# Decay rows as whole runs in DRAM, and a new work list for layer 1 of a two-layer hybrid trunk

## The chip, the cores and the metric

The kernel runs on one core of a Trainium2 chip. The metric is device time in microseconds (us), the median of several runs. A core has five engines with an instruction queue each: TensorE (PE) multiplies matrices into PSUM, VectorE (DVE) and ScalarE (ACT) do elementwise work, GpSimd (POOL) does elementwise work on SBUF alone, and SyncE (SP) here only issues DMAs. Every queue is worked off in order: an instruction that waits holds up all that stand behind it on its engine.

## What is computed

The reference runs 640 tokens (a prompt of 128 and a sample of 512) of width 1024 through two layers and a final norm. Each layer normalises, modulates by a condition, runs one mixer and adds its gated output to the stream.

```python
for i in range(DEPTH):
    ...
    hp = rms_norm(yp, norm_g[i]) * (1.0 + sc_p) + sh_p
    hs = rms_norm(ys, norm_g[i]) * (1.0 + sc_s) + sh_s
    if i % N_MIXERS == 0:
        out_p, out_s = conformer_branch(hp, False, *cw), conformer_branch(hs, True, *cw)
    else:
        out_p, s_f, s_b = ssd_branch(hp, zero_state, zero_state, *sw)
        out_s, _, _ = ssd_branch(hs, state_fwd[:, j], state_bwd[:, j], *sw)
    yp = yp + gt_p * out_p
    ys = ys + gt_s * out_s
```

Layer 1, where the change lies, is a Mamba-2 scan in both directions, in chunks of 128 tokens (one of the prompt, four of the sample) with 32 heads in 4 groups:

```python
a_cum = jnp.cumsum(la, axis=-1)
lower = jnp.tril(jnp.ones((CHUNK, CHUNK), dtype=bool))
seg = a_cum[..., :, None] - a_cum[..., None, :]
decay_mat = jnp.exp(jnp.where(lower, seg, -jnp.inf))
cb = jnp.einsum('bclgn,bcsgn->bcgls', cc, bc)
y_diag = jnp.einsum('bcgrls,bcsgrp->bclgrp', cb[:, :, :, None] * decay_mat, xdt)
chunk_states = jnp.einsum('bcsgn,bcgrs,bcsgrp->bcgrpn', bc, decay_to_end, xdt)
y_off = jnp.einsum('bclgn,bcgrpn,bcgrl->bclgrp', cc, prev, jnp.exp(a_cum))
```

The decay matrix needs, for each chunk and group, the running sum of every head as a row that all partitions see, and the same sum as a column.

## The kernel before

Layer 0 (the convolution branch) takes the first half of the time. Layer 1 then works through 38 projection tiles in an order that PLAN1 writes out: x (16 tiles, two of which layer 0 already does), B and C (4 each) and z (16). Each tile is 48 matmuls of 128x128 by 320 columns; the weights are split into a high and a low half to keep float32 accuracy, so each product is three matmuls. After its projection an x, B or C tile is evacuated by ScalarE, convolved with 5 taps (ScalarE the first, VectorE four), passed through SiLU and, for x and B, turned by TensorE so that tokens lie on partitions. Behind the projections the scan of a group starts: "group" needs B and the four x tiles of its group. Its chains in the two directions ("chain") multiply x by weights on GpSimd (xw), make a chunk's state on TensorE (pst), and add it to the state decayed by GpSimd (stn). Each chunk's output needs the product of C and B (pcb), the decay matrix (gf), their product on VectorE, TensorE's py, and the contribution of the states (po, yo). Gating by z, a split into halves (yh, yl), a sum of squares (ysq, ssp) and the output products follow; "o" items of PLAN1 are the output products of groups 0 to 2, and "last_products" those of group 3, followed by the final norm and the store.

The decay matrix is loaded rather than computed: the running sums of both directions lie in DRAM as acd, 128 rows (direction and head) by 384 columns. "decays" (L1575 to L1595) loads for each group and chunk 8 rows, spread over 64 partitions by a broadcast: gf takes 128 columns of each row, gb 64. So the pieces are 512 and 256 bytes long. There are four DMAs per chunk, 20 chunks in all. "decay" then subtracts a column from gb on GpSimd (L1567), copies half of it into gf under a mask on VectorE (L1569), and takes the exponential on ScalarE (L1573).

The order of all instructions of a layer is made when the program is built. Every chain of work is a generator that yields steps: "op" names an engine, a duration and the function that emits the instructions; "key" waits for another chain's mark; "get" and "put" take and return buffers of a ring. The class Order (L244) keeps a clock for each engine, picks among the chains' next steps the one that can begin first (with a priority per kind of chain, PRIO1, for ties), emits it and advances the clock. Some steps name two engines; the first way is taken at its time, the other with a bias:

```python
key = (t + 0.4 * load if len(ways) == 1 else t + dur - ways[0][1] + bias * n, ch[2], ch[3])
...
t = yield either((PO, 1.29, lambda: G.tensor_add(out=x_, in0=x_, in1=as_part(tmp, ch))), (VL, 0.66, lambda: V.tensor_add(out=x_, in0=x_, in1=as_part(tmp, ch))), bias=PRIO1["add_way"] * 0.2)
```

A step on SP counts as done LATE = 4.2 us after its issue. A clock for the transfers (DM) exists, and layer 1 does not use it. Rings say how many buffers there are: two for gf and gb each, six for the states (st).

Of the kernel before, what the change touches and what calls it, by code (L numbers as in the profile page):

```python
# [13 lines left out]
P = 128  # L14
# [36 lines left out]
def trunk(ctx: ExitStack, tc: tile.TileContext, a: dict):  # L51
# [194 lines left out]
    class Order:  # L246
        def __init__(self, prio):
            self.clock = [0.0] * 6
            self.table = None
            self.port = 0.0  # L250
            self.keys = {}
            self.rings = {}
            self.chains = []
            self.count = 0
            self.prio = prio
            self.same = [-OVER[e_] for e_ in range(5)]
            self.same.append(0.0)
            self.lead = MARGIN[PE]
            self.dirty = True
# [50 lines left out]
        def run(self, until=None):  # L310
            while self.chains:
# [26 lines left out]
                ch[1] = t + dur + LATE.get(eng, 0.0)  # L338
# [9 lines left out]
    LATE = {SP: 4.2}  # L348
# [828 lines left out]
    if True:  # L1177
# [22 lines left out]
        acd = dr.tile([P, 384], F32, name="acd")  # L1200
# [37 lines left out]
        def w_load(i, src, g=None):  # L1238
# [35 lines left out]
            t = yield op(SP, 0.35, load)  # L1274
# [57 lines left out]
        def convolve(ps, j, tag, bufs, name, cell, u=None):  # L1332
# [9 lines left out]
            for d in range(1, 5):  # L1342
                t = yield op(VL, 0.89, lambda: V.scalar_tensor_tensor(out=acc, in0=u[:, d : d + PW], scalar=c("w_c", j * 5 + d), in1=acc, op0=ALU.mult, op1=ALU.add))  # L1343
# [144 lines left out]
        def gate_loads():  # L1488
            yield key(("gated",))
            for g in range(3):  # L1490
                for hf in range(2):
# [7 lines left out]
                    t = yield op(SP, 0.6, load)  # L1499
# [12 lines left out]
            t = yield op(SP, 1.2, load_last)  # L1512
# [64 lines left out]
        def decays():  # L1577
            yield key(("cols",))
            for g in range(NG):
                for n, ch in enumerate(ORDER[g]):  # L1580
# [4 lines left out]
                    def load():  # L1585
# [3 lines left out]
                        for z_, n_, flip in ((gb, 64, True), (gf, 128, False)):  # L1589
                            for i in range(2):  # L1590
                                r, col = at(i != flip, ch, 8 * g)
                                col += 64 * (flip and i)
                                nc.sync.dma_start(out=z_[64 * i : 64 * i + 64].rearrange("p (h n) -> p h n", h=8), in_=acd[r : r + 8, col : col + n_].unsqueeze(0).broadcast_to([64, 8, n_]))
                    t = yield op(SP, 4.0, load)
                    start(decay(g, n, *tiles, t), t)  # L1595

        def group(g):
# [13 lines left out]
            for back, ch0, nm in ((0, 1, "st_f"), (1, 4, "st_b")):  # L1611
# [5 lines left out]
                t = yield op(SP, 0.4, load)  # L1617
# [43 lines left out]
            def prompt():  # L1661
                yield key(("pc", g, 0), ("st", g, 0, 4), ("st", g, 1, 3))
                for back in range(2):
# [10 lines left out]
                    t = yield op(SP, 0.1, lambda: nc.sync.dma_start(out=a["o_st"][back, g], in_=cell[1]))  # L1674
# [59 lines left out]
            for n, ch in enumerate(order):  # L1734
# [118 lines left out]
        def out_weights():  # L1853
# [13 lines left out]
            yield op(SP, 0.1, load)  # L1867
# [14 lines left out]
            t = yield op(SP, 0.3, load_gain)  # L1882
# [90 lines left out]
        def time_steps():  # L1973
# [47 lines left out]
        def rows_out():  # L2021
            yield op(SP, 0.1, lambda: nc.sync.dma_start(out=acd, in_=rp))
# [215 lines left out]
```

## Time and profile before

| | |
|---|---|
| runs | 1068.51, 1068.78, 1073.05 us; median 1068.78 |
| the profiled execution | 1068.35 us; its span from first to last instruction 1066.6 us |
| busy share of the span | PE 97%, PEld 89%, DVE 76%, ACT 62%, POOL 45% |
| matmuls | 7473 |
| DMA | 151.62 MB in 99162 packets, 29168 of them under 512 bytes |
| layer 1's projections on PE | from 544.9 us on |
| mean granted clock of TensorE | 0.991 |

The profile is of one execution. "Busy" sums the time in which an engine had an instruction in work; PE is matmul, PEld the load of its stationary operand, which overlaps. A matmul is shown from its start to the end of its way through the array, so its length is more than the distance to the next. A row of waits gives the waiting engine and line, what ended the wait, and then the total in us, the number of times and the longest. A row of DMA issues gives how long the queue took to issue; "landing" is from issue to the data's arrival. In a row of stretches each engine's busy us is followed by its number of instructions, and at the end stand TensorE's granted clock, the busy share of the 16 DMA engines and GB/s.

### The profile page before, as it was taken

Reading aid. Unit: us, or ns where it says so; the run is one execution under the profiler, and the core shown is the slowest. Engines: PE = TensorE matmul, PEld = TensorE weight load, DVE = VectorE, ACT = ScalarE, POOL = GpSimd, SP = SyncE. Lnnn points to the kernel's source line nnn. Section 1 sums busy time; section 2 is a strip of 40 time slices with the busy share of each in tenths; the row PEclk is TensorE's granted clock in tenths of the full one; section 3 lists DMA queues with packets and bytes.
Section 4 is the critical chain, followed back from the end, with each engine's and each line's share of the span. In section 5 each row is a group of like instructions: output and inputs, shape, how many; then the busy total and the mean of one; then the engine's idle time right before and its main releaser. Section 6 shows DMA issues by size and latency. Waiting matters only on the chain.

```text
span 1066.6 us, 19151 instructions
## 1 busy us (share of the span) xinstructions
PE 1033.6 (97%) x7473; PEld 948.5 (89%) x7473; DVE 807.8 (76%) x1214; ACT 666.5 (62%) x1109; POOL 478.1 (45%) x474
## 2 busy tenths in 40 slices
PE   6999999999999999999999999999999999999986
PEld 3899999999999999999999988997889778997665
DVE  2599999998997689103779788887769767965797
ACT  6468788787686678333587756774637533852454
POOL 0029999978596501111000147326561576006732
PEclk9999999999999999999999999999999999999988
DMA  9598788788766667675122753333553534335323
GB/s 359 195 256 206 190 218 198 178 210 210 176 141 137 141 136 155 150 168 123 60 76 61 156 120 103 86 101 84 144 138 98 120 88 120 84 109 134 97 69 92
DMA packets 99162, 151.62 MB, mean 142 GB/s; under 512 B 29168, under 2 KB 62336, under 8 KB 99072
## 3 DMA queue, kind: packets, MB, share of 16 engines
q1 hardware_dynamic: 87280, 118.15, 38.0%
q0 software_dynamic: 8640, 30.94, 17.3%
q10 hardware_dynamic: 3152, 1.31, 0.5%
q8 instruction: 59, 0.97, 0.4%
q14 instruction: 31, 0.25, 0.1%
HBM read 145.45 MB, written 4.92 MB: 141 GB/s over the span
## 4 chain that ended last, share of the span: by engine, by line
PE 88%; DVE 6%; DMA 2%; ACT 2%; issue 1%; SPq 0%; DVEq 0%; ACTq 0%
PE pz L1299 9%; PE o L1550 8%; PE xs L1299 7%; PE C L1299 3%; PE po L1692 3%; PE pst L1629 2%; PE B L1299 2%; PE py L1760 2%; PE o L1904 1%; PE o__4958 L157 1%; PE o__5245 L157 1%; PE o__5267 L157 1%; PE o__5258 L157 1%; PE o__5238 L157 1%; PE o__4948 L157 1%; DMA wa<-w_ada 1%
## 5 line engine op out<-in xcount | busy, mean ns | idle before, releaser
L809 DVE SCALAR_TENSOR_TENSOR cva<-v,cst,cva 128x550 f32<-128x550 f32 (+12 forms) x346 | 270.1, 821 | 11.4 <-ACT cva L801 6.3
L881 POOL TENSOR_TENSOR cv<-cv,tp 128x490 f32<-128x490 f32 (+5 forms) x134 | 172.6, 1288 | 8.5
L840 ACT ACTIVATE tp<-v,cst 128x490 f32<-128x490 f32 (+5 forms) x134 | 92.4, 718 | 36.3 <-POOL cv L881 35.9
L424 ACT CAST wh<-wf 128x1024 fp32r<-128x1024 f32 x63 | 65.9, 1046 | 63.5 <-PE o__5267 L157 30.0
L1299 PE MATMUL pz<-h_hi,wh 128*128 128x320 f32 x256 | 85.6, 334 | 0.8 <-ACT up L1330 0.8
L1299 PE MATMUL pz<-h_hi,wl 128*128 128x320 f32 x256 | 79.8, 312 | 0.1
L1299 PE MATMUL pz<-h_lo,wh 128*128 128x320 f32 x256 | 79.7, 311 | 0.0
L1529 POOL TENSOR_TENSOR x<-x,tmp 128x512 f32<-128x512 f32 x30 | 45.1, 1506 | 70.8 <-DVE tmp L1525 70.7
L1299 PE MATMUL xs<-h_hi,wh 128*128 128x320 f32 x224 | 76.0, 339 | 0.0
L1698 POOL TENSOR_TENSOR y<-y,yo 128x512 f32<-128x512 f32 x32 | 47.3, 1477 | 58.2 <-DVE yo L1696 51.4
L1573 ACT ACTIVATE gf<-gf,cols 128x128 f32<-128x128 f32 x160 | 50.8, 390 | 32.3 <-DVE gf L1569 32.2
L1343 DVE SCALAR_TENSOR_TENSOR xs<-up,cst,xs 128x642 f32<-128x642 f32 x64 | 62.9, 984 | 9.6 <-ACT xs L1341 7.9
L1299 PE MATMUL xs<-h_hi,wl 128*128 128x320 f32 x224 | 69.2, 309 | 0.0
L1299 PE MATMUL xs<-h_lo,wh 128*128 128x320 f32 x224 | 69.1, 308 | 0.0
L434 ACT ACTIVATE wl<-wh 128x1024 fp32r<-128x1024 f32 x58 | 61.5, 1061 | 1.7
L435 POOL DMA_DIRECT2D wl<-w_in x43 | 37.5, 872 | 54.8 <-ACT wl L434 51.6
L1256 DVE TENSOR_TENSOR wl<-wf,wh 128x1024 fp32r<-128x1024 f32 x38 | 49.9, 1317 | 15.5 <-ACT wh L1248 11.9
L1567 POOL TENSOR_TENSOR gb<-gb,cols 128x512 f32<-128x512 f32 x20 | 24.5, 1223 | 71.6 <-DVE C L1343 63.2
L1550 PE MATMUL o<-wh,yh 128*128 128x512 f32 x120 | 54.0, 450 | 0.0
L435 POOL DMA_DIRECT2D wl<-w_out x15 | 13.0, 865 | 90.4 <-ACT wl L434 90.4
L1299 PEld LDWEIGHTS pz<-h_hi,wh 128*128 128x128 f32 x256 | 48.6, 190 | 3.9 <-issue 2.6
L1299 PEld LDWEIGHTS pz<-h_lo,wh 128*128 128x128 f32 x256 | 48.8, 190 | 2.1 <-issue 1.9
(848 smaller groups left out, 3518.6 us busy)
## 6 DMA issues: line engine op xcount, KB each, us to landing
wf<-w_in SPq DMA_DIRECT2D x48, 512.0 KB, 3.8
wl<-w_in POOLq DMA_DIRECT2D x43, 512.0 KB, 7.3
wa<-w_ada SPq DMA_DIRECT2D x64, 256.0 KB, 6.0
wf<-w_out SPq DMA_DIRECT2D x32, 512.0 KB, 3.6
wf<-w_xbc SPq DMA_DIRECT2D x24, 512.0 KB, 4.0
gf<-acd SPq DMA_DIRECT2D x40, 256.0 KB, 4.9
wa<-w_ada SPq DMA_DIRECT2D x16, 512.0 KB, 10.2
wf<-w_z SPq DMA_DIRECT2D x16, 512.0 KB, 3.6
```

What stands on the lines that cost most here:

```text
L157: T.matmul(ps[:, b, at : at + t1 - t0], lhsT=w, rhs=h[:, t0:t1], start=first and n == 0, stop=last and n == 2)
L424: t = yield op(ACT, 1.05, lambda: S.copy(out=wh, in_=wf))
L434: yield op(ACT, 1.06, lambda: S.activation(out=wl, in_=wh.bitcast(F32), func=AF.Copy, scale=-1.0))
L435: t = yield op(PD, 0.7, lambda: G.dma_start(out=wl, in_=src, accum_op=ALU.add))
L809: t = yield op(VE, 0.24 + 0.01 * (hi - lo), lambda: V.scalar_tensor_tensor(out=rows64(accs[i], lo, hi), in0=rows64(vs[i], lo + d, hi + d), ...
L840: t = yield op(ACT, 0.72, lambda: S.activation(out=tp[:, :, 0 : hi - lo], in_=rows64(vs[i], lo + d, hi + d), func=AF.Copy, scale=w_dw(i, t ...
L881: t = yield op(PO, 1.3 + 0.019 * (hi - lo - 49), lambda: G.tensor_add(out=rows64(cv[i], lo, hi), in0=rows64(cv[i], lo, hi), in1=sgs["tp", ...
L1256: e_.tensor_sub(out=cell["wl"], in0=cell["wf"], in1=cell["wh"].bitcast(F32))
L1299: T.matmul(ps[:, b, at_ : at_ + t1 - t0], lhsT=w_, rhs=t_[:, t0:t1], start=k == 0 and n == 0, stop=k == nk - 1 and n == 2)
L1343: t = yield op(VL, 0.89, lambda: V.scalar_tensor_tensor(out=acc, in0=u[:, d : d + PW], scalar=c("w_c", j * 5 + d), in1=acc, op0=ALU.mult, ...
L1550: T.matmul(ps, lhsT=t_, rhs=w_, start=k == 0 and n == 0, stop=k == 3 and n == 2)
L1573: t = yield op(ACT, 0.39, lambda: S.activation(out=gv[:, h_, :], in_=gv[:, h_, :], func=AF.Exp, bias=cols1[ch][:, o8 + h_ : o8 + h_ + 1]), ...
```

## The change

The running sums are written to DRAM twice: acf holds three blocks (the chunk's place in a row) of 128 rows by 128 columns, acb three blocks of two halves of 128 rows by 64 columns. The 8 rows of a group are then one contiguous run of 4 KB in acf and of 2 KB in acb, and each partition's share of a load is one piece. Bytes and the number of loads stay; the one write becomes two.

Layer 1's list now uses the transfer clock: most loads name a time on it as a last argument, and the lateness of SP steps is 2.6 us in layer 1 (layer 0 keeps 4.2). A chunk's loads count 1.5 us on SP and 2.2 on the transfer clock, in the place of 4.0 us on SP. Several VectorE durations are raised (a convolution step from 0.89 to 0.97). The subtraction that makes the low half of a gained weight, two instructions, is listed as two steps. TensorE's margin is a knob and comes out as before, 0.2 x (-2 + 7) = 1.0 us. There is one buffer for gb, and seven for the states. All of PRIO1 and PLAN1 are new; they were chosen by replaying the finished order with scattered durations. Among the priorities, add_way goes from 5 to -3, so the bias of the residual adds goes from +1.0 to -0.6.

```diff
-PLAN1 = "z00 b0 z01 x03 x02 c0 x11 x10 z02 x13 x12 b1 x20 x23 z03 x22 z10 c1 b2 o00 z11 x33 o01 c2 z12 x21 z13 z20 b3 z30 o10 z21 o11 z22 z23 x30 x32 c3 x31 z31 o20 z32 o21 z33"
-RB1 = {"xs": 2, "st": 6, "gf": 2, "gb": 2}
+PLAN1 = "z00 b0 c0 z01 x02 x03 x13 b1 x10 x12 x22 x11 z02 x20 c1 x23 z03 b2 z10 x21 o00 z11 x33 o01 z12 z13 z20 c2 z30 x30 z21 x32 o10 z22 c3 z23 z31 o11 b3 x31 o20 z32 o21 z33"
+RB1 = {"xs": 2, "st": 7, "gf": 2, "gb": 1}
...
+            self.late = 4.2
...
-                ch[1] = t + dur + LATE.get(eng, 0.0)
+                ch[1] = t + dur + (self.late if eng == SP else 0.0)
                 if table and eng != ACT:
                     self.clock[DM] = max(self.clock[DM], t + 0.3) + table
                     ch[1] = max(ch[1], self.clock[DM] + (2.2 if eng == SP else -3.6))
...
-        acd = dr.tile([P, 384], F32, name="acd")
+        acf = dr.tile([3, P, 128], F32, name="acf")
+        acb = dr.tile([3, 2, P, 64], F32, name="acb")
...
-                    t = yield op(VL, 1.55, lambda: low(V))
+                    yield op(VL, 0.77, lambda: low(V))
+                    t = yield op(VL, 0.77, lambda: low(V, 1))
...
-            t = yield op(SP, 0.35, load)
+            t = yield op(SP, 0.35, load, 1.35)
...
-                        for z_, n_, flip in ((gb, 64, True), (gf, 128, False)):
-                            for i in range(2):
-                                r, col = at(i != flip, ch, 8 * g)
-                                col += 64 * (flip and i)
-                                nc.sync.dma_start(out=z_[64 * i : 64 * i + 64].rearrange("p (h n) -> p h n", h=8), in_=acd[r : r + 8, col : col + n_].unsqueeze(0).broadcast_to([64, 8, n_]))
-                    t = yield op(SP, 4.0, load)
+                        for i in range(2):
+                            r, col = at(1 - i, ch, 8 * g)
+                            nc.sync.dma_start(out=gb[64 * i : 64 * i + 64], in_=acb[col // 128, i, r : r + 8, :].rearrange("h n -> (h n)").unsqueeze(0).broadcast_to([64, 512]))
+                        for i in range(2):
+                            r, col = at(i, ch, 8 * g)
+                            nc.sync.dma_start(out=gf[64 * i : 64 * i + 64], in_=acf[col // 128, r : r + 8, :].rearrange("h n -> (h n)").unsqueeze(0).broadcast_to([64, 1024]))
+                    t = yield op(SP, 1.5, load, 2.2)
...
-            yield op(SP, 0.1, lambda: nc.sync.dma_start(out=acd, in_=rp))
+            yield op(SP, 0.4, lambda: nc.sync.dma_start(out=acb.rearrange("c f p n -> p c f n"), in_=rp.rearrange("p (c f n) -> p c f n", c=3, f=2)), 1.0)
+            yield op(SP, 0.4, lambda: nc.sync.dma_start(out=acf.rearrange("c p n -> p c n"), in_=chunks(rp)), 0.8)
...
-            run.clock = [0.0, -2.0, -2.0, -2.0, -9.0]
+            run.clock = [0.0, -2.0, -2.0, -2.0, -9.0, -9.0]
+            run.lead = 0.2 * (PRIO1["lead"] + 7)
+            run.late = 2.6
```

More of the change, by code (lines that the diff above doesn't have):

```diff
@@ L1251, in high, with low @@
                         S.activation(out=cell["wh"][:, z_], in_=cell["wf"][:, z_], func=AF.Copy, scale=sn)
-            def low(e_):
-                cell["wl"] = gp.tile([P, 1024], F32R, tag="wl", bufs=3, name="wl")
+            def low(e_, n=0):
+                if n == 0:
+                    cell["wl"] = gp.tile([P, 1024], F32R, tag="wl", bufs=3, name="wl")
                 if g is None:
@@ L1257, in low @@
                 else:
-                    for z_, sn in gained(g, cell):
-                        e_.scalar_tensor_tensor(out=cell["wl"][:, z_], in0=cell["wf"][:, z_], scalar=sn, in1=cell["wh"][:, z_].bitcast(F32), op0=ALU.mult, op1=ALU.subtract)
+                    (z_, sn), = gained(g, cell)[n : n + 1]
+                    e_.scalar_tensor_tensor(out=cell["wl"][:, z_], in0=cell["wf"][:, z_], scalar=sn, in1=cell["wh"][:, z_].bitcast(F32), op0=ALU.mult, op1=ALU.subtract)
             def split():
@@ L1279, in gained @@
         def gained(g, cell):
-            for n in range(2):
-                yield slice(n * 512, n * 512 + 512), c("sn_g", g + n)
+            return [(slice(n * 512, n * 512 + 512), c("sn_g", g + n)) for n in range(2)]
         def w_chain():
@@ L1342, in convolve @@
             for d in range(1, 5):
-                t = yield op(VL, 0.89, lambda: V.scalar_tensor_tensor(out=acc, in0=u[:, d : d + PW], scalar=c("w_c", j * 5 + d), in1=acc, op0=ALU.mult, op1=ALU.add))
+                t = yield op(VL, 0.97, lambda: V.scalar_tensor_tensor(out=acc, in0=u[:, d : d + PW], scalar=c("w_c", j * 5 + d), in1=acc, op0=ALU.mult, op1=ALU.add))
             up_free(u, t)
@@ L1673, in prompt @@
                     put("b", t)
-                    t = yield op(SP, 0.1, lambda: nc.sync.dma_start(out=a["o_st"][back, g], in_=cell[1]))
+                    t = yield op(SP, 0.35, lambda: nc.sync.dma_start(out=a["o_st"][back, g], in_=cell[1]))
                     put("st", t)
@@ L1743, in group @@
                 cbd = lp.tile([P, 1], F32, tag="cbd", bufs=2, name="cbd")
-                yield op(VE, 0.4, lambda: V.scalar_tensor_tensor(out=pcb[:, 128:256], in0=pcb[:, 0:128], scalar=1.0, in1=eye, op0=ALU.mult, op1=ALU.mult, accum_out=cbd))
+                yield op(VE, 0.3, lambda: V.scalar_tensor_tensor(out=pcb[:, 128:256], in0=pcb[:, 0:128], scalar=1.0, in1=eye, op0=ALU.mult, op1=ALU.mult, accum_out=cbd))
                 co = lp.tile([P, 8], F32, tag="co", bufs=2, name="co")
-                t = yield op(VL, 0.25, lambda: V.scalar_tensor_tensor(out=co, in0=cols2[ch][:, 96 + o8 : 104 + o8], scalar=cbd, in1=c("d", o8, 8), op0=ALU.mult, op1=ALU.add))
+                t = yield op(VL, 0.36, lambda: V.scalar_tensor_tensor(out=co, in0=cols2[ch][:, 96 + o8 : 104 + o8], scalar=cbd, in1=c("d", o8, 8), op0=ALU.mult, op1=ALU.add))
                 start(other_y(ch, co, n), t)
@@ L1866, in out_weights @@
             yield get("wf")
-            yield op(SP, 0.1, load)
+            yield op(SP, 0.35, load, 1.35)
             for k in range(2):
```

15 lines of the change are left out of this document (7 added, 8 removed).

## The prediction

> **What bounds the kernel now.** I read the page first, then the busy time by stretches, then TensorE's waits in the part that the change touches.
>
> ```profile
> span 1066.6 us, 19151 instructions
> PE 1033.6 (97%) x7473; PEld 948.5 (89%) x7473; DVE 807.8 (76%) x1214; ACT 666.5 (62%) x1109; POOL 478.1 (45%) x474
> ```
>
> ```profile
> core 0: us, PE busy (x) PEld busy (x) DVE busy (x) ACT busy (x) POOL busy (x), PEclk, DMA share, GB/s
> 1057.90:1066.60 8.70, 0.00 (x0) 0.00 (x0) 2.96 (x6) 2.37 (x6) 1.27 (x1) 0.66 0.43 121
> 0.00:545.00 545.00, 533.14 (x4409) 514.51 (x4409) 400.94 (x608) 363.99 (x540) 264.09 (x309) 1.00 0.71 176
> 545.00:1000.00 455.00, 449.06 (x2813) 395.72 (x2814) 348.13 (x496) 268.56 (x495) 187.62 (x144) 1.00 0.42 109
> 1000.00:1067.00 67.00, 51.41 (x254) 38.24 (x252) 58.69 (x112) 33.90 (x75) 26.35 (x22) 0.90 0.33 91
> ```
>
> TensorE is the bound, and the span splits at 545 us, where layer 1's list begins. From there to 1000 us TensorE is idle for 455.00 - 449.06 = 5.9 us. From 1000 us on it is idle for 15.6 us, of which 8.7 us lie behind its last matmul (the final norm and the store), so 6.9 us are gaps; its clock there is 0.90. All that a better list can win lies in these gaps and in that clock. The waits name them:
>
> ```profile
> PE ssp L1830 <- DVE ysq L1825: 2.6, 2, 1.4
> PE ptx L1367 <- ACT xs L1345: 1.2, 1, 1.2
> ```
>
> ```profile
> PE ssp L1830 <- DVE ysq L1825: 1.5, 1, 1.5
> PE pst L1629 <- DVE yo L1696: 1.3, 1, 1.3
> PE py L1760 <- DVE gf L1751: 1.2, 2, 0.6
> PE ssp L1830 <- ACT ss L1838: 1.2, 1, 1.2
> PE pcb L1740 <- ACT xt L1730: 0.7, 1, 0.7
> ```
>
> The first two rows are from 545 to 1000 us, the other five from 1000 us on. No row names a DMA: the transfers that the change speeds up reach TensorE only through VectorE or ScalarE.
>
> **The change part by part.**
>
> *Layer 0* keeps its priorities, plan and lateness of 4.2: no change up to 545 us.
>
> *The decay transfers.* Four DMAs per chunk, twenty chunks:
>
> ```profile
> L1593 SPq DMA_DIRECT2D gb<-acd x40: 580/621/1307, 597.9 to 1011.2; - x40
> L1593 SPq DMA_DIRECT2D gf<-acd x40: 573/626/1713, 599.3 to 1012.5; - x40
> L2022 SPq DMA_DIRECT2D acd<-room x1: 327/327/327, 578.0 to 578.0; - x1
>   POOL gb L1567: 8.4, 6
>   ACT L1573: 5.3, 2
> DMA to landing us min/median/max: 1.9/4.9/9.8
> ```
>
> ```profile
> 597.00:611.00 14.00, 14.00 (x99) 13.93 (x98) 9.59 (x13) 9.58 (x19) 1.32 (x2) 1.00 0.99 197
> 956.00:962.00 6.00, 6.00 (x28) 4.82 (x27) 1.55 (x3) 0.27 (x1) 3.23 (x3) 1.00 0.47 175
> ```
>
> ```profile
> L1243 SPq DMA_DIRECT2D wf<-w_z x15: 327/333/2846, 545.5 to 972.3; - x15
> ```
>
> GpSimd and ScalarE waited 8.4 and 5.3 us for these landings. In the stretch with two decay chunks the DMA engines are full (0.99) and move 197 GB/s, so 199 GB/s at a share of one. In the second stretch, where only whole rows of 2 and 4 KB move, it is 175 / 0.47 = 372 GB/s. A chunk is 2 x 256 + 2 x 128 = 768 KB: 3.95 us at the first rate, 2.11 at the second, so 1.8 us less. The issue falls from 0.62 to about the 0.33 to 0.43 us of transfers by whole rows; I take 0.38, so 4 x 0.24 = 1.0 us per chunk. Together a chunk lands about 2.8 us earlier (estimate; from 1.0, if 64 reads of one row gain nothing, to 2.8). The SP time saved, 20 us in all, is time in which SP otherwise waits: no gain by itself. On TensorE's path I find it in one place:
>
> ```profile
> 599.95 7.72 DMA gf<-acd
> 622.67 0.66 PE ptx L1367 x4
> ```
>
> The chain of waits runs through the first chunk's landing of 7.72 us into VectorE's convolution and from there into the 1.2 us wait of ptx. I take the whole 1.2 us off; bounds 0 and 2.4 (with the 1.2 us of py on gf).
>
> Writing the rows takes two DMAs in the place of one (0.33 us, 1.9 us to land at 578.0). The first read starts at 597.9: 18 us of cover, cost nothing; without it, about 2 us. One gb buffer for two adds a wait on SP for the copy out of gb. Behind it stand weight loads; their consumer has three split tiles in hand, 3 x 7.04 = 21 us of TensorE work, against a delay of some 5 us in the pair of chunks at 598 us: nothing, else those 5 us. A seventh state buffer costs nothing on any engine.
>
> *The list's durations.* The old list counts 0.89 us for a convolution step and 4.0 + 4.2 us for a chunk's loads; the new one 0.97, and 0.3 + 2.2 + 2.2 = 4.7 us by its transfer clock:
>
> ```profile
> L1343 DVE SCALAR_TENSOR_TENSOR xs<-up,cst,xs 128x642 f32<-128x642 f32 x64 | 62.9, 984 | 9.6 <-ACT xs L1341 7.9
> ```
>
> The row says 0.984 us; 64 such steps are 6 us of drift that the old list did not see, and the ssp waits, where TensorE's in-order queue meets a VectorE result that is late, are of this kind. Of the idle 5.9 us, 4.7 us are left after ptx. All of it or as many new waits are the bounds (-4.7 and +4.7); I take half off, -2.3, since new orders make waits of their own. All other priorities of layer 1 and the plan are redrawn too; an order can't be priced piece by piece, so it goes into this term and its bounds. Splitting the gained weights' subtraction in two costs nothing: it was two instructions already.
>
> *Residual adds.* Their bias between GpSimd and VectorE goes from +1.0 to -0.6. VectorE's 0.63 us shorter add now wins unless GpSimd could start 1.23 us sooner.
>
> ```profile
> L1529 POOL TENSOR_TENSOR x<-x,tmp 128x512 f32<-128x512 f32 x30 | 45.1, 1506 | 70.8 <-DVE tmp L1525 70.7
> L1918 DVE TENSOR_TENSOR x<-x,tmp 128x512 f32<-128x512 f32 x10 | 8.8, 884 | 0.3
> ```
>
> ```profile
> 760.00:800.00 40.00, 40.00 (x234) 31.99 (x234) 29.48 (x43) 17.67 (x32) 23.91 (x17) 1.00 0.48 119
> 840.00:880.00 40.00, 40.00 (x213) 31.10 (x214) 24.44 (x36) 15.63 (x32) 26.43 (x22) 1.00 0.55 123
> 960.00:1000.00 40.00, 40.00 (x209) 31.34 (x208) 22.39 (x34) 11.75 (x22) 30.04 (x25) 1.00 0.43 109
> 1000.00:1040.00 40.00, 33.85 (x176) 24.33 (x175) 39.23 (x75) 23.01 (x48) 19.21 (x17) 0.91 0.33 91
> ```
>
> Up to 30 x 0.88 = 27 us move onto VectorE. In three of the stretches with output products VectorE has 10.5, 15.6 and 17.6 us free: hidden. Only behind 1000 us, at 39.2 of 40, would each add cost its 0.88 us.
>
> *The end.* Group 3's scan starts when its last x tile (x31) is projected, convolved and turned. Before, z31 o20 z32 o21 z33 follow it in the plan; now o20 z32 o21 z33: one projection less to cover group 3's chain.
>
> ```profile
> 938.44 7.04 PE xs L1299 x48
> ```
>
> ```profile
> 957.14 0.27 ACT L1369 COPY xt<-ptx 128x128 f32<-128x128 f32 x1 [1.86 <-PE ptx L1367]
> ```
>
> ```profile
> 957.17 1.30 POOL L1529 TENSOR_TENSOR x<-x,tmp 128x512 f32<-128x512 f32 x1 [46.85 <-DVE tmp L1525]
> ...
> 966.99 2.05 POOL L1624 TENSOR_TENSOR xw<-xt,cols 128x512 f32<-128x512 f32 x2
> ```
>
> That tile less is +7.0 us if the chain keeps its length. But the chain has slack: x31 is ready at 957.4, and GpSimd begins group 3's first product xw at 967.0, behind four residual adds and a state decay. With the adds on VectorE, xw can begin 967.0 - 957.4 = 9.6 us sooner. I take 7.0 - 9.6 = -2.6 us; bounds +7.0, and -10.5: all 6.9 us of gaps, and 40 x (1 - 0.91) = 3.6 us of clock.
>
> *What clock is lost* shows in two products of one shape:
>
> ```profile
> 1026.11 0.63 PE L1904 MATMUL o<-wl,yh 128*128 128x512 f32 x1
> 1027.50 0.39 PE L1904 MATMUL o<-wh,yl 128*128 128x512 f32 x1
> ```
>
> The longest wait ahead of it was 1.5 us. [...]
>
> *Sum.* Against the profiled execution's 1068.35 us: -1.2 (transfers) - 2.3 (durations) - 2.6 (end) = -6.1, so 1062.2; the median of the runs stands 0.4 above that execution: **1062.7 us**.
>
> **The rivals.**
>
> *The end loses its cover (slower).* Group 3 gains nothing on GpSimd because the state loads or VectorE hold it, and the missing tile is paid: 1068.8 + 7.0 = 1075.8. For it: VectorE is full from 1000 us on. Against it: 17.6 us free just ahead. It decides if first xw comes more than 2.6 us after x31's last copy (9.6 - 7.0).
>
> *Nothing on the path.* The transfers were hidden but for ptx, and the new order trades waits one for one: 1068.8 - 1.2 = 1067.6. For it: no DMA among TensorE's waits, and only 12.8 us of gaps in all. Against it: rows that contradict the old list's durations.
>
> *The end closes up.* All gaps from 1000 us on and the clock: 1068.8 - 1.2 - 2.3 - 10.5 = 1054.8. For it: five different waits there, each on an engine that was ordered by wrong times. Against it: VectorE at 39.2 of 40.
>
> *Only gb gains.* If 512-byte pieces run as fast as whole rows, only a third of the 1.8 us and the 1.0 us of issue are saved: 1.6 of 2.8 us. A chunk then lands at 3 x 0.62 + 4.9 - 1.6 = 5.2 us where the list counts on 4.7; 0.5 us late on each of group 3's last three chunks makes 1062.7 + 1.5 = 1064.2. [...]
>
> **How the numbers follow.** Forecast 0.43 (its own range 1058 to 1067), nothing on the path 0.23, the end loses its cover 0.16, the end closes up 0.13, only gb gains 0.05. The time is the forecast's. The unknown costs reach from 1068.8 - 2.4 - 4.7 - 10.5 = 1051.2 to 1068.8 + 4.7 + 7.0 = 1080.5; leaving out the outer parts of both far cases gives 1054 to 1076. What a measurement can tell from no change is 0.5%, 5.3 us: below 1063.5 is faster, above 1074.1 slower. Faster takes 0.31 of the forecast, the closing end, and 0.02 of the last case: 0.46. Slower is most of the lost cover: 0.15. The rest is 0.39.
>
> **What would show it.** Layer 0 ends at 545 us again. gb and gf issue in under 0.45 us and land 2 to 3 us sooner after the first issue; a stretch with two chunks exceeds 300 GB/s per full share. The POOL adds of L1529's line fall from 30 to under 12, VectorE's rise by as many. First xw of group 3 follows x31's last copy by under 2.6 us. TensorE's gaps before 1000 us are under 4 us, and its clock behind 1000 us is above 0.90. The forecast is wrong if the gaps keep their sum, or if the gaps behind z33 grow by more than the others shrink.

## The result, and the profile after

The changed kernel takes 1062.12 us (median of four runs, 1061.39 to 1063.33) against 1069.01 for the kernel before: a ratio of 0.993 with a 95% interval of 0.990 to 0.996. The forecast was 1062.7. The profiled execution took 1061.69 us. Its page, and its busy time by stretches:

```profile
span 1059.8 us, 19157 instructions
PE 1031.0 (97%) x7473; PEld 946.4 (89%) x7473; DVE 827.0 (78%) x1240; ACT 667.0 (63%) x1112; POOL 440.0 (42%) x443
```

```profile
core 0: us, PE busy (x) PEld busy (x) DVE busy (x) ACT busy (x) POOL busy (x), PEclk, DMA share, GB/s
545.00:1000.00 455.00, 452.05 (x2846) 398.94 (x2846) 374.83 (x527) 268.56 (x498) 150.90 (x116) 1.00 0.38 112
545.70:1001.50 455.80, 453.50 (x2854) 400.16 (x2855) 375.17 (x528) 269.22 (x499) 152.40 (x117) 1.00 0.38 112
1001.50:1051.60 50.10, 44.61 (x213) 32.38 (x211) 47.32 (x100) 30.77 (x70) 22.47 (x18) 0.93 0.27 74
```

The last two rows cut layer 1 where it matters: from its first projection to the last matmul of the last projection (I call it the dense part), and from there to TensorE's last matmul (the tail). The kernel before, cut in the same way:

```profile
544.90:1006.90 462.00, 456.02 (x2854) 401.97 (x2855) 355.03 (x505) 270.24 (x500) 192.33 (x148) 1.00 0.43 110
1006.90:1057.90 51.00, 44.51 (x213) 32.06 (x211) 48.92 (x98) 29.95 (x67) 20.37 (x17) 0.93 0.28 73
```

Both cuts hold the same number of matmuls, 2854 and 213, in the two kernels. The dense part goes from 462.0 to 455.8 us (-6.2), the tail from 51.0 to 50.1 (-0.9), what lies behind the last matmul from 8.7 to 8.2 (-0.5), and layer 1 starts 0.8 us later, since layer 0's end moves a little from execution to execution. That is the span's -6.8. Inside the dense part TensorE's idle time falls from 462.00 - 456.02 = 6.0 us to 2.3, and its busy time for the same matmuls by 2.5 us. The waits that are left on TensorE, first from 545 to 1000 us (pz's 1.7 us ends at 545.7, where the dense part begins, and is no part of its idle time), then the longest behind that:

```profile
PE pz L1301 <- ACT up L1332: 1.7, 1, 1.7
PE ssp L1833 <- DVE ysq L1828: 1.6, 1, 1.6
PE ssp L1833 <- DVE ss L1837: 0.4, 1, 0.4
PE pty L1722 <- POOL y L1701: 0.3, 1, 0.3
```

```profile
PE ssp L1833 <- DVE ysq L1828: 2.1, 1, 2.1
PE py L1763 <- issue: 1.6, 1, 1.6
```

The 1.2 us wait of ptx is gone, and with it a longer one that the prediction does not name, at 580 us in the kernel before:

```profile
PE pt L2046 <- DVE room L1982: 1.5, 1, 1.5
```

These two and 0.6 us less of ssp (2.0 for 2.6) are nearly all of the 3.7 us of idle time that the dense part lost. The decay transfers (issue in ns: shortest, median, longest) and the residual adds:

```profile
L1593 SPq DMA_DIRECT2D gb<-acb x40: 444/486/1332, 602.6 to 1003.0; - x40
L1596 SPq DMA_DIRECT2D gf<-acf x40: 444/591/1012, 603.8 to 1006.3; - x40
```

```profile
L1531 DVE TENSOR_TENSOR x<-x,tmp 128x512 f32<-128x512 f32 x30 | 25.4, 847 | 1.0
```

All thirty adds that GpSimd did are on VectorE.

### The profile page after: what moved, and what is told of

Its sections match the earlier page's. It is cut to its first block, busy times and chain, and to the rows that moved or that the text cites. A ratio compares the mean times of both kernels' runs of the same rounds, so it can differ in the third digit from the quotient of the medians.

```text
span 1059.8 us, 19157 instructions
## 1 busy us (share of the span) xinstructions
PE 1031.0 (97%) x7473; PEld 946.4 (89%) x7473; DVE 827.0 (78%) x1240; ACT 667.0 (63%) x1112; POOL 440.0 (42%) x443
## 4 chain that ended last, share of the span: by engine, by line
PE 88%; DVE 5%; ACT 2%; DMA 2%; issue 2%; SPq 0%; POOL 0%; DVEq 0%; ACTq 0%; POOLq 0%
PE pz L1301 9%; PE xs L1301 8%; PE o L1552 8%; PE B L1301 2%; PE C L1301 2%; PE po L1695 2%; PE pst L1632 2%; PE o L1907 2%; PE py L1763 2%; PE o__4958 L157 1%; PE o__5267 L157 1%; PE o__5258 L157 1%; PE o__5245 L157 1%; PE o__4948 L157 1%; PE o__5238 L157 1%
## 5 line engine op out<-in xcount | busy, mean ns | idle before, releaser
L424 ACT CAST wh<-wf 128x1024 fp32r<-128x1024 f32 x63 | 65.9, 1047 | 63.4 <-PE o__5267 L157 29.8
L1701 POOL TENSOR_TENSOR y<-y,yo 128x512 f32<-128x512 f32 x32 | 49.8, 1555 | 85.1 <-DVE yo L1699 81.5
L1345 DVE SCALAR_TENSOR_TENSOR xs<-up,cst,xs 128x642 f32<-128x642 f32 x64 | 66.3, 1037 | 10.2 <-ACT xs L1343 8.8
L1575 ACT ACTIVATE gf<-gf,cols 128x128 f32<-128x128 f32 x160 | 50.8, 391 | 29.8 <-DVE gf L1571 29.7
L1249 ACT CAST wh<-wf 128x1024 fp32r<-128x1024 f32 x38 | 39.5, 1046 | 18.5 <-DMA wf<-w_xbc 6.1
```

What stands on the lines that cost most here:

```text
L424: t = yield op(ACT, 1.05, lambda: S.copy(out=wh, in_=wf))
L1345: t = yield op(VL, 0.97, lambda: V.scalar_tensor_tensor(out=acc, in0=u[:, d : d + PW], scalar=c("w_c", j * 5 + d), in1=acc, op0=ALU.mult, ...
L1575: t = yield op(ACT, 0.39, lambda: S.activation(out=gv[:, h_, :], in_=gv[:, h_, :], func=AF.Exp, bias=cols1[ch][:, o8 + h_ : o8 + h_ + 1]), ...
```

## The experiments

The changed kernel was run once more beside the first three experiments (e1, e2, e3), as their control. The others were run at other times, beside the kernel before alone, so across them only the ratios compare.

> The changed kernel once more, beside the next three on one chip: 0.993 of the kernel before (0.990 to 0.996), about 1062 us. It is the measure for them.

Layer 0's end lies between 543.8 and 548.5 us in these runs, so its jitter hides small effects in the span. Layer 1's own length, from the start of its first projection to TensorE's last matmul, has less: 505.9 us in the changed kernel, 505.4 when it was profiled again, 513.0 in the kernel before. I use it beside the ratios; it comes from one profile of each run. Here all runs stand together; "idle" is the dense part less TensorE's busy time in it, in us:

| run | ratio to before, 95% | layer 1 | dense part | idle in it | tail |
|---|---|---|---|---|---|
| before | 1 | 513.0 | 462.0 | 6.0 | 51.0 |
| after (again) | 0.9935, 0.9919 to 0.9952 | 505.4 | 455.9 | 2.3 | 49.5 |
| e1_old_rows | 0.9935, 0.9916 to 0.9955 | 506.3 | 456.8 | 2.9 | 49.5 |
| e2_rows_alone | 1.0004, 0.9990 to 1.0018 | 513.2 | 462.4 | 6.2 | 50.8 |
| e9_distinct | 0.9951, 0.9937 to 0.9964 | 505.9 | 456.0 | 2.4 | 49.9 |
| e3_adds_gpsimd | 0.9956, 0.9940 to 0.9973 | 508.6 | 459.1 | 4.2 | 49.5 |
| e4_z31_late | 1.0028, 1.0016 to 1.0041 | 514.1 | 464.7 | 4.8 | 49.4 |
| e5_old_knobs | 1.0097, 1.0072 to 1.0122 | 520.0 | 466.6 | 8.4 | 53.4 |
| e6_old_model | 1.0096, 1.0076 to 1.0116 | 522.5 | 470.6 | 11.5 | 51.9 |
| n1_step98 | 1.0051, 1.0030 to 1.0072 | 520.5 | 471.2 | 11.5 | 49.3 |
| n2_step96 | 0.9982, 0.9969 to 0.9995 | 508.5 | 458.9 | 4.1 | 49.6 |
| n3_late27 | 0.9932, 0.9910 to 0.9953 | 505.7 | 456.1 | 2.3 | 49.6 |
| e10_warm | 0.9942, 0.9924 to 0.9959 | 505.5 | 456.0 | 2.4 | 49.5 |

### The rows: out of the new list, and into the old one

*e1_old_rows* keeps the new list word for word and reads the running sums as before, in pieces of 512 and 256 bytes.

```diff
-        acf = dr.tile([3, P, 128], F32, name="acf")
-        acb = dr.tile([3, 2, P, 64], F32, name="acb")
+        acd = dr.tile([P, 384], F32, name="acd")
...
+                        for z_, n_, flip in ((gb, 64, True), (gf, 128, False)):
...
-            yield op(SP, 0.4, lambda: nc.sync.dma_start(out=acf.rearrange("c p n -> p c n"), in_=chunks(rp)), 0.8)
+            yield op(SP, 0.4, lambda: None, 0.8)
```

> The changed kernel with the running sums in DRAM as before (one write, pieces of 512 and 256 bytes), the list kept instruction for instruction. Theory 1 (the order carries the gain, the transfers reach TensorE in one place only): at most 1.5 us slower than the changed kernel, some 1063 us. Theory 2 (the transfers carry it, since the list counts on an early landing): each chunk's last landing comes 1.5 to 3 us later and the time goes back by 4 us or more, to 1066 us and up. Landing of gf back to 4.9 us from 4.2.

*e2_rows_alone* is the kernel before, its list included, with the new layout and its loads.

```diff
-                                nc.sync.dma_start(out=z_[64 * i : 64 * i + 64].rearrange("p (h n) -> p h n", h=8), in_=acd[r : r + 8, col : col + n_].unsqueeze(0).broadcast_to([64, 8, n_]))
+                            nc.sync.dma_start(out=gb[64 * i : 64 * i + 64], in_=acb[col // 128, i, r : r + 8, :].rearrange("h n -> (h n)").unsqueeze(0).broadcast_to([64, 512]))
...
+                            nc.sync.dma_start(out=gf[64 * i : 64 * i + 64], in_=acf[col // 128, r : r + 8, :].rearrange("h n -> (h n)").unsqueeze(0).broadcast_to([64, 1024]))
```

> The kernel before with the new rows alone (two writes, pieces of 2 and 4 KB), its list kept. Theory 1: 0 to 1.5 us faster than the kernel before, 1067.5 to 1069 us, since that list places the consumers behind a landing it takes to be 8.2 us away. Theory 2: 3 us or more faster.

With the old rows the changed kernel is as fast, 0.9935 like the control beside it; with the new rows the old kernel stays at 1.0004. The rows are worth nothing that the ratios can show, and their intervals reach some 2 us to either side: with them layer 1 is 0.4 or 0.9 us shorter in the new list (505.9 and 505.4 for 506.3) and 0.2 us longer in the old one. The issues show how little the transfers changed. First the changed kernel (size of one, median us from issue to landing), then its list with the old rows:

```profile
gf<-acf SPq DMA_DIRECT2D x40, 256.0 KB, 4.2
gb<-acb SPq DMA_DIRECT2D x40, 128.0 KB, 3.3
```

```profile
gf<-acd SPq DMA_DIRECT2D x40, 256.0 KB, 4.8
gb<-acd SPq DMA_DIRECT2D x40, 128.0 KB, 3.5
L1594 SPq DMA_DIRECT2D gf<-acd x40: 573/628/653, 602.7 to 1006.1; - x40
```

In one and the same list pieces eight times as long land 0.6 us (gf) and 0.2 us (gb) sooner; in the old list, e2 against the kernel before, it is 0.5 and 0.4. The issue of gf falls only from 0.63 to 0.59 us, that of gb from 0.60 to 0.49. The same 6 us from a chunk's first load on, with long pieces and with short ones:

```profile
975.00:981.00 6.00, 6.00 (x36) 4.31 (x35) 5.58 (x10) 0.01 (x1) 3.22 (x5) 1.00 0.85 219
```

```profile
974.70:980.70 6.00, 6.00 (x36) 4.31 (x36) 5.58 (x10) 0.04 (x1) 3.28 (x4) 1.00 1.01 217
```

The long pieces keep the DMA engines busy for less (0.85 against 1.01) and move 219 GB/s against 217: per full share 258 against 215, with hardly more bytes moved in the same time. The short wait of ptx, on which I had put 1.2 us of gain, is absent with the old rows too; these are TensorE's waits in that stretch:

```profile
PE ssp L1831 <- DVE ysq L1826: 1.6, 1, 1.6
PE py L1761 <- DVE gf L1752: 0.7, 1, 0.7
PE ssp L1831 <- DVE ss L1835: 0.4, 1, 0.4
PE pty L1720 <- POOL y L1699: 0.3, 1, 0.3
```

So the new order takes ptx's wait away without the new transfers. The transfers alone halve it: in e2 0.6 us of it are left, but the waits of ssp grow from 2.6 to 3.5 us there, and the dense part is no shorter. What the old rows cost in the new list is the 0.7 us of py on gf, a wait that the changed kernel doesn't have.

*e9_distinct* asks whether the loads stay slow because 64 partitions read one and the same row. It reads 64 different rows of a weight in pieces of the same sizes, and takes the exponential with a scale of zero, so that every decay is one.

```diff
-                t = yield op(ACT, 0.39, lambda: S.activation(out=gv[:, h_, :], in_=gv[:, h_, :], func=AF.Exp, bias=cols1[ch][:, o8 + h_ : o8 + h_ + 1]), "exp")
+                t = yield op(ACT, 0.39, lambda: S.activation(out=gv[:, h_, :], in_=gv[:, h_, :], func=AF.Exp, scale=0.0, bias=nil[:, 0:1]), "exp")
...
-                            nc.sync.dma_start(out=gb[64 * i : 64 * i + 64], in_=acb[col // 128, i, r : r + 8, :].rearrange("h n -> (h n)").unsqueeze(0).broadcast_to([64, 512]))
+                            nc.sync.dma_start(out=gb[64 * i : 64 * i + 64], in_=a["w_xbc"][5 * g + n, 64 * i : 64 * i + 64, 0:512])
...
-                            nc.sync.dma_start(out=gf[64 * i : 64 * i + 64], in_=acf[col // 128, r : r + 8, :].rearrange("h n -> (h n)").unsqueeze(0).broadcast_to([64, 1024]))
+                            nc.sync.dma_start(out=gf[64 * i : 64 * i + 64], in_=a["w_xbc"][5 * g + n, 64 * i : 64 * i + 64, :])
```

> The changed kernel with gb and gf loaded from 64 different rows of a weight tensor, in pieces of the same 2 and 4 KB, in the place of one row read 64 times; the exponential takes zero in the place of the decays, so all decays are one. It measures what the repeated row costs. If reading one row many times is what holds the landing of gf at 4.2 us: 3 us or less, and the DMA engines at 350 GB/s or more per full share in the stretch with two loads. If it is the queue: 4 us again. Time within 1 us of the changed kernel either way.

```profile
gf<-w_xbc SPq DMA_DIRECT2D x40, 256.0 KB, 4.0
gb<-w_xbc SPq DMA_DIRECT2D x40, 128.0 KB, 3.0
```

The landing is 0.2 to 0.3 us shorter; gf's issue is the same (0.59 us) and gb's no shorter (0.57 for 0.49). Reading one row 64 times is not what holds these loads; about 4 us is what a load of 256 KB took behind its neighbours here, whatever it read.

### The residual adds back on GpSimd

The list stays that of the changed kernel; only the engine that does the adds of the thirty steps is GpSimd again.

```diff
-            t = yield either((PO, 1.29, lambda: G.tensor_add(out=x_, in0=x_, in1=as_part(tmp, ch))), (VL, 0.66, lambda: V.tensor_add(out=x_, in0=x_, in1=as_part(tmp, ch))), bias=PRIO1["add_way"] * 0.2)
+            t = yield either((PO, 1.29, lambda: G.tensor_add(out=x_, in0=x_, in1=as_part(tmp, ch))), (VL, 0.66, lambda: G.tensor_add(out=x_, in0=x_, in1=as_part(tmp, ch))), bias=PRIO1["add_way"] * 0.2)
```

> The changed kernel with the residual adds that its list gives to VectorE carried out by GpSimd, at the same places of the list. If the adds on VectorE were what let group 3's scan run sooner (my step on the end): xw of group 3 again stands behind them and the time goes up by 2 to 5 us. If their engine makes no difference: within 1 us of the changed kernel.

Layer 1 grows by 2.7 us against 505.9, the time by 2.2 us against the control beside it (1065.0 and 1062.8). Where it grows speaks against my reason for it. GpSimd's rows around the place where x31 has been turned:

```profile
961.66 0.27 ACT L1371 COPY xt<-ptx 128x128 f32<-128x128 f32 x1 [1.62 <-PE ptx L1369]
...
962.45 1.29 POOL L1531 TENSOR_TENSOR x<-x,tmp 128x512 f32<-128x512 f32 x1 [1.95 <-DVE tmp L1527]
965.35 1.74 POOL L1531 TENSOR_TENSOR x<-x,tmp 128x512 f32<-128x512 f32 x1 [1.60 <-DVE tmp L1527]
968.51 1.49 POOL L1627 TENSOR_TENSOR xw<-xt,cols 128x512 f32<-128x512 f32 x1
```

```profile
949.30:972.90 23.60, 23.60 (x127) 20.43 (x126) 15.50 (x18) 8.40 (x15) 12.32 (x8) 1.00 0.40 122
972.90:1005.10 32.20, 31.26 (x162) 23.07 (x161) 23.49 (x32) 9.87 (x20) 27.21 (x23) 1.00 0.47 132
1005.10:1054.60 49.50, 44.34 (x213) 31.96 (x211) 47.07 (x100) 30.83 (x70) 22.33 (x17) 0.93 0.27 75
```

The first product xw comes 968.5 - 961.9 = 6.6 us after x31's last copy, well past the 2.6 us from which I let the end lose its cover. It did not lose it. The three rows are cut at x31's last projection matmul, group 3's first state (pst), the last projection matmul and the last matmul. The changed kernel, cut in the same way, has 23.60, 30.80 and 50.10 us: the first state comes exactly as soon, the tail is no longer, and 1.4 us are lost between, 0.9 us of them idle. Another 1.9 us lie before x31, and the tail gives 0.6 back. GpSimd was a cause, but not the one that sets when group 3 begins.

### z31 behind x31 again

```diff
-PLAN1 = "z00 b0 c0 z01 x02 x03 x13 b1 x10 x12 x22 x11 z02 x20 c1 x23 z03 b2 z10 x21 o00 z11 x33 o01 z12 z13 z20 c2 z30 x30 z21 x32 o10 z22 c3 z23 z31 o11 b3 x31 o20 z32 o21 z33"
+PLAN1 = "z00 b0 c0 z01 x02 x03 x13 b1 x10 x12 x22 x11 z02 x20 c1 x23 z03 b2 z10 x21 o00 z11 x33 o01 z12 z13 z20 c2 z30 x30 z21 x32 o10 z22 c3 z23 o11 b3 x31 z31 o20 z32 o21 z33"
```

> The changed kernel with the projection z31 moved behind x31 again in the plan (as in the kernel before), the list made anew from that plan. Theory 1 (group 3's scan runs sooner than the projections behind x31 could be missed): within 2 us of the changed kernel, 1060.5 to 1065 us. Theory 2 (the cover is worth its 7 us and the changed kernel lost it): 3 to 7 us faster, 1056 to 1060 us.

```profile
546.10:1010.80 464.70, 459.94 (x2881) 404.31 (x2881) 378.93 (x535) 271.47 (x507) 157.43 (x122) 1.00 0.38 112
1010.80:1060.20 49.40, 40.27 (x186) 30.88 (x185) 42.57 (x94) 27.69 (x61) 13.36 (x12) 0.86 0.21 54
```

```profile
PE ssp L1833 <- ACT ss L1841: 4.5, 1, 4.5
PE py L1763 <- issue: 4.4, 1, 4.4
```

Layer 1 is 8.2 us longer, 514.1 against 505.9. With the tile's cover back, 27 more matmuls of the scan are done before the last projection (2881 for 2854), and yet the tail is as long as ever, 49.4 us, now with two new waits of 4.5 and 4.4 us. This run remade the whole list, so it prices the plan with its remade list and not the tile alone. In this one list the tail did not shrink when group 3's chain was given more time ahead of it; but the two waits and 13.65 us at a clock of 0.50 (1015.05 to 1028.70) fill it, with VectorE busy for only 42.6 us, so it doesn't show what the cover is worth in a good order.

### The parts of the list: model, knobs, neighbours

*e5_old_knobs* has the new rows, durations and transfer clock, with the plan, the priorities and the rings of before. *e6_old_model* has the new rows, plan, priorities and rings, with the durations and the lateness of before. Both cuts are against the changed kernel; in e5 all of PRIO1 changes too.

```diff
...
-RB1 = {"xs": 2, "st": 7, "gf": 2, "gb": 1}
...
+PLAN1 = "z00 b0 z01 x03 x02 c0 x11 x10 z02 x13 x12 b1 x20 x23 z03 x22 z10 c1 b2 o00 z11 x33 o01 c2 z12 x21 z13 z20 b3 z30 o10 z21 o11 z22 z23 x30 x32 c3 x31 z31 o20 z32 o21 z33"
+RB1 = {"xs": 2, "st": 6, "gf": 2, "gb": 2}
```

> The changed kernel (rows, durations, transfer clock) with the plan, the priorities and the buffer counts of the kernel before. If the truer durations make the order better by themselves: 1063 to 1067 us. If the choice of plan and priorities is what gains: 1068 us or more, and group 3's adds are on GpSimd again.

```diff
-                t = yield op(VL, 0.97, lambda: V.scalar_tensor_tensor(out=acc, in0=u[:, d : d + PW], scalar=c("w_c", j * 5 + d), in1=acc, op0=ALU.mult, op1=ALU.add))
+                t = yield op(VL, 0.89, lambda: V.scalar_tensor_tensor(out=acc, in0=u[:, d : d + PW], scalar=c("w_c", j * 5 + d), in1=acc, op0=ALU.mult, op1=ALU.add))
...
-                    t = yield op(SP, 1.5, load, 2.2)
+                    t = yield op(SP, 4.0, load)
```

> The kernel before's durations and lateness, with the plan, the priorities, the buffer counts and the rows of the changed kernel. If plan and priorities carry the gain whatever the durations: 1061 to 1064 us. If they only fit the durations they were chosen with: 1067 us or more.

Each half alone is slower than the kernel before, by 0.97% and 0.96%. Truer durations gain nothing by themselves, nor do the new plan and priorities with the old durations. In e6 TensorE's new waits before 1000 us are on VectorE's sum and on an evacuation by ScalarE:

```profile
PE ssp L1832 <- DVE ss L1836: 4.9, 2, 4.6
PE B L1300 <- ACT zs L1422: 3.6, 1, 3.6
```

So I asked how special the one list is. *n1_step98* and *n2_step96* count a convolution step as 0.98 and 0.96 us in the place of 0.97, and let the list be made again; *n3_late27* counts SP's lateness as 2.7 us for 2.6, which leaves the finished order as it was but for one turn of three matmuls on TensorE.

```diff
-                t = yield op(VL, 0.97, lambda: V.scalar_tensor_tensor(out=acc, in0=u[:, d : d + PW], scalar=c("w_c", j * 5 + d), in1=acc, op0=ALU.mult, op1=ALU.add))
+                t = yield op(VL, 0.98, lambda: V.scalar_tensor_tensor(out=acc, in0=u[:, d : d + PW], scalar=c("w_c", j * 5 + d), in1=acc, op0=ALU.mult, op1=ALU.add))
```

> The changed kernel with one duration of its list changed by 0.01 us: a convolution step counts 0.98 in the place of 0.97; plan, priorities, buffers and rows stay, the list is made anew. If the truer model with this plan and these priorities is what gains, a neighbour is as good: within 2 us of the changed kernel, 1060 to 1065 us. If the gain is this one list, picked from many: a neighbour falls back by 4 us or more, to 1066 to 1078 us.

> The neighbour on the other side: a convolution step counts 0.96. Model and plan: 1060 to 1065 us. One picked list: 1066 to 1078 us.

```diff
-            run.late = 2.6
+            run.late = 2.7
```

> SP's lateness in layer 1's list is 2.7 us in the place of 2.6. The finished order is then that of the changed kernel but for one place: on TensorE one turn of the gate rows (pt, three products) stands three matmuls later; the four other engines' orders are the same word for word. If the scatter of the two neighbours (1074.8 and 1066.2 us for 0.01 us more or less in one duration) comes from the orders themselves, this one must agree with the changed kernel: layer 1 from first projection to last matmul 505 to 507 us, time 1061.5 to 1064, ratio to the kernel before 0.992 to 0.996. If any touch of the list makes the chip run it several us worse (data placement, buffer addresses, issue of the queues), it comes out at 1066 or more.

One hundredth of a microsecond in one duration makes layer 1 14.6 us longer in n1 and 2.6 in n2 (by the ratios 12 and 5 us behind the control, each to within some 4 us); n3 reproduces the changed kernel, 505.7 us. So it is the order, not the touch, that costs. The dense part of n1, and the place of its deepest loss:

```profile
546.10:1017.30 471.20, 459.71 (x2854) 404.46 (x2855) 371.75 (x528) 265.00 (x497) 152.38 (x117) 0.99 0.38 108
906.68:910.09 3.41, 1.17 (x7) 0.77 (x5) 3.38 (x6) 0.00 (x0) 2.11 (x1) 1.00 0.19 50
910.09:916.92 6.83, 5.85 (x31) 5.51 (x32) 2.04 (x5) 5.09 (x12) 1.26 (x1) 0.50 0.55 177
```

The same 2854 matmuls have 9.2 us more idle time (11.5 for 2.3) and 6.2 us more busy time, of which 10.2 us at half the clock (831.58 to 834.99 and 910.09 to 916.92) explain at most 5.1.

### The clock in the tail

In the changed kernel the tail holds one stretch of 6.83 us at half clock:

```profile
1008.63:1012.04 3.41, 0.85 (x6) 0.64 (x6) 3.34 (x11) 2.99 (x5) 1.29 (x1) 1.00 0.61 178
1012.04:1018.87 6.83, 6.17 (x25) 4.45 (x26) 6.80 (x15) 1.73 (x3) 2.04 (x2) 0.50 0.02 4
```

Output products of 128x512 begin every 0.43 us at its end (1017.33 to 1018.61) and every 0.23 us behind it (from 1018.97 on).

*e10_warm* puts idle products in front of it, eight ahead of group 3's first ssp and six ahead of its fourth py, into PSUM columns that are overwritten or not read.

```diff
+        def warm(out, n):
+            for _ in range(n):
+                T.matmul(out, lhsT=eye, rhs=eye, start=True, stop=True)
...
+                    if g == 3 and n == 3:
+                        warm(py[:, 0:128], 6)
...
+                if g == 3 and not warmed:
+                    warmed.append(ch)
+                    warm(ps[:, 128:256], 8)
```

> The changed kernel, its list kept, with 14 matmuls of 128 columns that compute nothing needed put in front of two TensorE waits of group 3 (8 ahead of the first ssp, 6 ahead of the fourth py), where it sat idle for 2.1 and 1.6 us before the clock fell to half for 6.8 us. If short waits that add up take the clock (my reading of the profile before): the clock stays, 1.5 to 3.4 us faster than the changed kernel. If the clock falls anyway: 0 to 1 us slower.

```profile
1003.40:1052.90 49.50, 45.76 (x240) 33.41 (x239) 47.08 (x99) 30.82 (x70) 22.29 (x18) 1.00 0.27 75
```

The clock reads 1.00 in the whole tail, and the tail is as long as in the other runs, 49.5 us; the gain of 1.5 to 3.4 us that I had expected did not come. Runs without idle products agree: with 6.83 us at half clock the tail is 49.5 to 50.1 us (the changed kernel, e1, e3, e9, n3), with some 3.4 us (a mean clock of 0.97) it is 49.5 and 49.6 (the changed kernel profiled again, n2). So the 3.4 us of clock (6.83 x 0.50) that the changed kernel loses there cost it nothing. In the changed kernel and in e10 the last run of sixty output products waits for VectorE's tmp, and it begins 36.0 and 35.4 us into the tail, whatever the clock was ahead of it (1037.47 - 1001.50 and 1038.75 - 1003.40). VectorE is busy for 47.1 of e10's 49.5 us. That the chain through VectorE sets the tail's length is read from this; no run changed VectorE's work there.

## Why the prediction was right, and where it was not

The total was right to 0.6 us, and that is luck. Two of its three terms had the wrong reason (transfers and end); they promised 3.8 us together, and the end gave 1.4. By place, the dense part's idle time gave 3.7 us, its busy time 2.5 and the end 1.4, and the later start of layer 1 took 0.8 back.

**Layer 0** ended at 545.7 us, as said; later runs show 543.8 to 548.5 from execution to execution.

**The decay transfers (-1.2)** are wrong. I let the rate go from 199 to 372 GB/s per full share and the issue to 0.38 us; measured are 258 GB/s, 0.49 us (gb) and 0.59 us (gf). Against the kernel before gf lands 0.7 us sooner and gb 1.6, not a chunk 2.8 us sooner, and part of that is the list's: in one list it was 0.6 and 0.2, in the other 0.5 and 0.4. The price came from a row of other transfers (whole rows, spread differently), which said nothing of a load that fills 64 partitions. My rival "only gb gains", 1064.2, took 512-byte pieces to run as fast as whole rows, which no row of the kernel before showed; then gf had nothing to gain and gb, in 256-byte pieces, had. Where only the rows differ, the landings go the other way: gf gained 0.6 and 0.5 us, gb 0.2 and 0.4. The rival also fails on its other step, that a late chunk costs its lateness three times: with the old rows e1's gf lands 0.6 us later, and one wait of 0.7 us is all that reaches TensorE before 1000 us. The bound "0" that I kept for this term was its value, within what the ratios can tell.

**The list's durations (-2.3)** had the right place, and of the two things that were won there they counted one. The dense part's idle time fell by 3.7 us, 2.5 without ptx's 1.2; that this is near the 2.3 is chance, as half of the idle time was a guess. What I had left out is the busy time, 2.5 us less, and the clock before 1000 us in it. In the kernel before one 1.4 us wait of ssp was followed by a stretch at a granted clock of 0.50:

```profile
695.52:698.93 3.41, 2.03 (x14) 1.87 (x14) 3.34 (x9) 2.57 (x5) 0.74 (x2) 1.00 0.84 148
698.93:702.34 3.41, 3.41 (x15) 3.37 (x14) 3.34 (x6) 2.19 (x4) 0.63 (x1) 0.50 0.04 11
```

Matmuls of 128x320 begin every 0.27 us in the stretch (from 698.94 on) and every 0.15 us ahead of it and behind it. By the clock the 3.41 us at 0.50 are 1.7 of the 2.5 us, by that distance 1.5 (3.41 x (1 - 0.147 / 0.267)); the other 0.8 to 1.0 are not explained. The second profile of the old list, e2, has such a stretch behind the same wait (700.08 to 703.49), and none of the six profiles of the new order has one in its dense part. I counted only the clock behind 1000 us, where e10 shows it to be free, and none before, where TensorE is the bound (busy for all 3.41 us of that stretch) and the loss counts. The row of 545 to 1000 us read 1.00, since 1.7 us in 455 disappear in the rounding of its last figure. As a cause, "truer durations" is too simple: e5 has them and is slower. The runs support only this: the gain belongs to the one finished order, and orders made in the same way a hundredth of a microsecond away are 2.6 and 14.6 us longer. That it was found by replays fits this, but no run here compares that choice with another way of choosing. I had said that an order can't be priced piece by piece and gave the term ±4.7 us; e5 and e6, 10.4 and 10.3 us slower than the kernel before by their ratios, show that ±10 was the honest bound.

**The residual adds** left GpSimd, all thirty (I had said under twelve would stay), and VectorE hid them in the dense part, as said.

**The end (-2.6)** is the step whose mechanism failed. I charged the moved tile 7.0 us and gave back 9.6 us from GpSimd's earlier start. GpSimd did start earlier, 2.3 us after x31's last copy:

```profile
959.43 0.27 ACT L1371 COPY xt<-ptx 128x128 f32<-128x128 f32 x1 [1.62 <-PE ptx L1369]
...
962.02 1.04 POOL L1627 TENSOR_TENSOR xw<-xt,cols 128x512 f32<-128x512 f32 x1
```

But group 3's first state came at 970.7, 23.6 us after x31's last projection matmul, where it had been 23.9 us before: TensorE's order held it, not GpSimd, and TensorE was full from x31 to the last projection in both kernels. From x31's last projection matmul to the first state and from there to the last projection matmul, first before, then after:

```profile
945.50:969.40 23.90, 23.90 (x132) 21.07 (x131) 11.30 (x16) 9.95 (x18) 8.53 (x8) 1.00 0.19 68
969.40:1006.90 37.50, 37.50 (x205) 29.58 (x204) 26.28 (x38) 10.64 (x23) 27.52 (x23) 1.00 0.56 148
```

```profile
947.10:970.70 23.60, 23.60 (x128) 20.41 (x127) 15.37 (x24) 8.41 (x15) 2.76 (x3) 1.00 0.42 131
970.70:1001.50 30.80, 30.80 (x162) 23.11 (x161) 25.95 (x36) 9.78 (x19) 20.69 (x17) 1.00 0.48 130
```

Together they are 7.0 us shorter and hold 47 matmuls less: the moved tile (48 matmuls, 7.04 us) and nothing else, with one record between. Moved out of a stretch in which TensorE is full, into another in which it is full, it cost nothing and gained nothing here. The tail behind the last projection is 49.3 to 51.0 us in all the lists but e5 and e6 (53.4 and 51.9). So the cover that I priced at 7.0 us was spare in this order, the rival "the end loses its cover" had no ground at the point I gave it (e3 passes that point at 6.6 us and stays in the tail's band), and the measured end is -0.9 - 0.5 = -1.4 us.

**"The end closes up"** was not near: the tail's gaps and clock are mostly not on the path. Its 3.6 us for the clock have a measured price of nothing.

**The signs to look for**: the gaps before 1000 us (2.95 us, under 4), the adds, and xw (2.3 us, under 2.6) came as written; the issue (under 0.45), the landing (2 to 3 us) and the rate (over 300) did not; the clock behind 1000 us, 0.91, was above 0.90 but proved nothing.

## What to carry to other kernels

Cut a bound engine's time where its work changes its limit (here the last projection matmul), count the same instructions on both sides, and split the difference into idle and busy time: this showed in two rows that 6.2 of the 6.8 us were won ahead of the last projection, while the sum by steps had spread them over transfers and the end. Before a lost clock, a late transfer or a missing cover is priced, look whether the engine that pays for it is the bound at that place; three of my prices fell on that. Where a static order is remade, give its term a bound from neighbours of the order, not from the idle time that is left.

## What the runs showed of the hardware

Layer 1's length is reproducible to about 1 us for one finished order (505.4 to 506.3 us in six profiles of it, with the old rows, other rows, idle products and three matmuls moved), while neighbouring orders differ by up to 14.6 us.

The stretches at a granted clock of 0.50 last 3.41 us in the dense part of the kernel before, 6.83 in the changed kernel's tail, 10.24 in e5's (a tail with a mean clock of 0.90) and 13.65 in e4's (0.86): one to four times 3.41. The longest waits ahead of the two shown were of 1.4 and 2.1 us: TensorE was busy for 2.03 of the 3.41 us ahead of the one at 698.9 us and for 0.85 ahead of the one at 1012.0. In the kernel before the stretch began 2.0 us behind the end of the 1.4 us wait; in the changed kernel none followed a wait of 1.6 us at the same sum (ssp). In the changed kernel profiled again the same waits of 2.1 (ssp) and 1.6 us (py) stand in the tail, and its clock reads 0.97 where it had read 0.93; in e10, whose waits there are of 0.9 us at most, it reads 1.00. What takes the clock, and when, no run here shows.

Two things were not tried. gb was not given its second buffer back with this list, so the price of SP's waits for it (13 of them, up to 8.7 us, none of which reaches TensorE's list of waits) is not measured by itself. And which of the changed waits make the one order good was not isolated.
